# The mean-square sums of an MLP's norm are issued earlier, and rstd and the copies of values out of PSUM get the priority of evacuations

## The chip, the cores and the metric

The kernel runs on one core of a Trainium2 chip. A core has five engines with instruction queues of their own, each served strictly in order: TensorE (PE; its weight loads are shown as PEld), VectorE (DVE), ScalarE (ACT), GpSimd (POOL) and SyncE (SP). They meet only at semaphores. TensorE writes its results to PSUM; VectorE and ScalarE carry them from there to SBUF (an "evacuation"). The metric is the device time of one execution in microseconds, lower is better.

## The reference

Two request groups share one set of weights: a context pass of 128 tokens and a denoising step of 512. The kernel handles them as T = 640 columns. There are two layers (L = 2), D = 1024, and each layer is

```
h = rmsnorm(x, g_attn) * (1 + scale1) + shift1
q, k, v, gq, gk, gv, gate, zf, zb = split(h @ w_in)
o_na  = attention(q, k, v)                 # neighbourhood window and cached context
o_gla = gla(gq, gk, gv, zf, zb)            # gated linear attention, both directions
x = x + gate1 * (concat(o_na, rmsnorm(o_gla) * silu(gate)) @ w_o)
h = rmsnorm(x, g_mlp) * (1 + scale2) + shift2
x = x + gate2 * (relu(h @ w_up) ** 2 @ w_down)

rmsnorm(x, g) = x * rsqrt(mean(x * x) + eps) * g
```

The factor rsqrt(mean(x * x) + eps) of a token is called rstd below. Arithmetic is float32: each operand of a large product is split into a high and a low part (`wh`, `wl` for weights; two tiles per slice of activations), and three matmuls stand for one.

## The kernel before, in words

Activations lie with features on the 128 partitions and the 640 tokens in the free dimension; x is eight slices `kc` of [128, 640]. Weights come in units of [128, 1024] through a few SBUF buffers: a DMA, ScalarE's copy to `wh`, and the subtraction to `wl` on VectorE or GpSimd (`prefetch`, `prepare`).

**What sets the order.** TensorE's program is in the order in which the code issues it. A small driver (`Drv`) interleaves tasks: the main loop is a `filler` that yields after each slice of a projection, and side tasks (generators) run between its steps. A task can yield a time in us or a claim on buffers ("sm", 2); `Drv` counts TensorE's estimated time `t` and runs a task when its time has come. `Est` keeps estimates of when other engines will have written a tile, and `est.until(tile)` is the estimated rest of that time plus 0.60. The other engines are ordered by a scheduler that takes instructions by priority; `tc.high_priority(offset=self.EVP)` with EVP = 600 moves what is issued inside it ahead of work issued up to 600 places earlier, as far as dependencies allow. Evacuations of projections are issued like that.

**PSUM.** The pool "mm" has two buffers of two banks (`ps_mm`), the pool "sm" four of one bank (`ps_sm`, `ps_ss`). An accumulation can begin only when a buffer's last reader is done.

**The norm before the MLP** (lines 881 to 926). Each finished slice of x goes through `late_chunk`: it is multiplied by a per-feature factor G and split in two parts (`row`, `m`), and its square is added to `lsqa` (in rows: `sqa`). The factor rstd is applied only behind the up projection: `late_stat` sums `lsqa` over the partitions by two matmuls with ones (`ps_ss`), and ScalarE makes rstd by Ln and Exp (`lrstd`, in rows `rstd`). Meanwhile `proj_two` runs the first two up units side by side through both `ps_mm` buffers: for each slice kc six matmuls of the one and six of the other (called a block each, below); behind the last slices comes the evacuation `r<-ps_mm,rstd`, which needs rstd. The third up unit needs a `ps_mm` buffer.

In layer 1 the up units from the fourth on are computed by a scheme of seven half-size products for a pair of units (`proj_pair`), which needs sums of blocks of h: `blocks_begin` (line 1655) makes them on VectorE and ScalarE just then (in rows `r<-r`, `T`, `row<-r,row`; "the block sums").

**The attention's values** (`v_task`, lines 1389 to 1415). Behind each of four value projections p, ScalarE writes `gt`, TensorE transposes it into one `ps_sm` buffer (four transposes) and then into another (two), and VectorE copies both to `V`: one 128x512 copy and two of 64x128. Beside that runs `gla_pair`, whose levels 64, 32, 16, 8, 4, 2, 1 each need a pair of factors from `level_vec` (VectorE: two subtractions `ex<-PN`; ScalarE: an exponential; VectorE: a product `ex<-ex,qk`), 80 small matmuls into two or four `ps_sm` buffers (`ps_sm<-ex`), and copies from there (`A`, `Dg`). Both share the four "sm" buffers. In layer 0, VectorE also carries the modulation's matrix-vector products (`junk<-wr,cbc`, `wr<-wr,cbc`).

All instructions of the engines are recorded by one helper, so that rows of the profile name line 198; they are told apart by tiles.

Of the kernel before, what the change touches and what calls it, by code (L numbers as in the profile page):

```python
# [12 lines left out]
AF = mybir.ActivationFunctionType  # L13
# [5 lines left out]
D = 1024  # L19
T = 640  # L20
# [192 lines left out]
class Kern:  # L213
# [684 lines left out]
    def late_chunk(self, x, kc, rows):  # L898
        nc = self.nc
        hh, hl = rows[kc]  # L900
        for r, a, b in ((1, 0, NS), (0, NS, T)):
            g = self.G[:, kc, r:r + 1]
            nc.scalar.activation(out=hh[:, 2 + a:2 + b], in_=x[kc][:, a:b], func=AF.Copy, scale=g)
            nc.vector.scalar_tensor_tensor(out=hl[:, 2 + a:2 + b], in0=x[kc][:, a:b], scalar=g, in1=hh[:, 2 + a:2 + b].bitcast(F32),
                                           op0=ALU.mult, op1=ALU.subtract)
        if kc == 0:
            nc.scalar.activation(out=self.lsqa, in_=x[kc], func=AF.Square)
        else:
            sq = self.npl.tile([128, T], F32, name="sq")
            nc.scalar.activation(out=sq, in_=x[kc], func=AF.Square)  # L910
            nc.vector.tensor_tensor(out=self.lsqa, in0=self.lsqa, in1=sq, op=ALU.add)
        if kc == KC - 1:
            self.dv.spawn(self.late_stat(), self.est.until(self.lsqa) + 3.0)

    def late_stat(self):
        nc, dv = self.nc, self.dv
        yield ("sm", 2)
        ps = [self.smp.tile([128, 512], F32, name="ps_ss", tag="sm") for _ in range(2)]
        for t, (lo, hi) in zip(ps, self.HALF):
            nc.tensor.matmul(t[:, 0:hi - lo], lhsT=self.ones, rhs=self.lsqa[:, lo:hi], start=True, stop=True)  # L920
        dv.pe(1.07)
        for t, (lo, hi) in zip(ps, self.HALF):
            nc.scalar.activation(out=self.lrstd[:, 2 + lo:2 + hi], in_=t[:, 0:hi - lo], func=AF.Ln, scale=1.0 / D, bias=self.eps)
        dv.rel("sm", 2, self.est.free(*ps))
        nc.scalar.activation(out=self.lrstd[:, 2:2 + T], in_=self.lrstd[:, 2:2 + T], func=AF.Exp, scale=-0.5)
        self.lready = True


# [460 lines left out]
    def v_task(self, l, p, ps):  # L1389

        nc, gp, dv = self.nc, self.gp, self.dv
        t = gp.tile([128, T], F32, name="gt", tag="tmp", bufs=5)
        nc.scalar.activation(out=t[:, :NS].rearrange("p (c r) -> p c r", r=8),
                             in_=ps[0][0][:, :NS].rearrange("p (r c) -> p c r", r=8), func=AF.Copy)
        nc.scalar.activation(out=t[:, NS:T], in_=ps[0][0][:, NS:T], func=AF.Copy)
        nc.scalar.dma_start(out=self.o["new_v"][l, p], in_=t[:, NS:T])
        yield self.est.until(t)
        yield ("sm", 1)
        pt = self.smp.tile([128, 512], F32, name="ps_sm", tag="sm")
        for i in range(3):  # L1400
            nc.tensor.transpose(pt[:, 128 * i:128 * i + 128], t[:, 64 + 128 * i:192 + 128 * i], self.ident)
        nc.tensor.transpose(pt[:, 384:512], t[:, NS:T], self.ident)
        dv.pe(0.43)
        nc.vector.tensor_copy(self.V[:, 0:4, 128 * p:128 * p + 128], pt.rearrange("p (c d) -> p c d", c=4))
        dv.rel("sm", 1, self.est.free(pt))
        yield ("sm", 1)
        pt = self.smp.tile([128, 512], F32, name="ps_sm", tag="sm")
        nc.tensor.transpose(pt[:, 0:128], t[:, 0:128], self.ident)
        nc.tensor.transpose(pt[:, 128:256], t[:, 384:512], self.ident)
        dv.pe(0.22)  # L1410
        for i, hs in enumerate((slice(0, 64), slice(64, 128))):
            nc.vector.tensor_copy(self.V[hs, 4, 128 * p:128 * p + 128], pt[hs, 128 * i:128 * i + 128])
        dv.rel("sm", 1, self.est.free(pt))
        dv.rel("gt")

# [486 lines left out]
```

## Time and profile before

| | |
|---|---|
| median of 3 runs | 1676.16 us (1676.02 to 1676.85) |
| the profiled execution's own time | 1676.12 us |
| its span, first to last instruction | 1674.3 us |
| TensorE busy, matmuls / weight loads | 1609.2 us (96%) / 1538.1 us (92%) |
| VectorE busy | 1226.0 us (73%) |
| ScalarE busy | 749.1 us (45%) |
| GpSimd busy | 388.8 us (23%) |
| mean granted TensorE clock | 0.990 of full speed |

The table gives shares of the whole. It says that TensorE is nearly always at work, and not where it waits; for that one reads the table of waits and then the timeline of the places it names. In the timeline a row is a run of like instructions: start, length, engine, line, operation, tiles, count, and in brackets the idle time of the engine before it and what ended that.

### The profile page before, as it was taken

How to read it: one execution, taken by the hardware profiler on the slowest of the kernel's cores; microseconds unless marked ns; L12 is line 12 of the kernel's file. 1: busy time of each engine (PE TensorE's matmuls, PEld its weight loads, DVE VectorE, ACT ScalarE, POOL GpSimd, SP SyncE). 2: the span in 40 equal slices, each digit the busy share in tenths (PEclk: the TensorE clock that was granted, in tenths of full speed). 3: DMA queues.
4: the chain of work that ended last, by engine and by line, in shares of the span. 5: the costliest groups of instructions: out<-in, count | busy, mean ns of one | idle time of the engine just before them, and what ended most of it. 6: DMA issues, size and time to landing. Idle time of an engine off the chain costs nothing. (4 is left out here: it accounts for less than half of the span.)

```text
span 1674.3 us, 32585 instructions
## 1 busy us (share of the span) xinstructions
PE 1609.2 (96%) x13544; PEld 1538.1 (92%) x13544; DVE 1226.0 (73%) x2318; ACT 749.1 (45%) x1224; POOL 388.8 (23%) x155
## 2 busy tenths in 40 slices
PE   8999899999999999999999998999979999999998
PEld 6988788879999999999998898988979999999998
DVE  5697978888888778777578867578695565665753
ACT  4546345644523323332355373566465344343441
POOL 1100000013344444444300000000222334243341
PEclk9999999999999999999999999999999999999999
DMA  9122242433554445444251111313111223222232
GB/s 373 57 81 79 99 150 76 134 112 99 183 164 140 150 149 166 134 132 151 82 186 51 57 52 50 104 61 108 51 55 60 79 73 101 65 87 76 76 94 84
DMA packets 61347, 179.28 MB, mean 107 GB/s; under 512 B 6928, under 2 KB 17808, under 8 KB 61200
## 3 DMA queue, kind: packets, MB, share of 16 engines
q1 hardware_dynamic: 45360, 159.76, 28.7%
q10 hardware_dynamic: 15840, 17.45, 3.4%
q8 instruction: 107, 1.75, 0.4%
q14 instruction: 40, 0.33, 0.1%
HBM read 170.36 MB, written 6.82 MB: 106 GB/s over the span
## 5 line engine op out<-in xcount | busy, mean ns | idle before, releaser
L198 POOL TENSOR_TENSOR wl<-wr,wh 128x1024 fp32r<-128x1024 f32 (+1 forms) x138 | 375.1, 2724 | 1219.6 <-ACT wh L198 1219.6
L198 PE MATMUL ps_mm<-row,wh 128*128 128x256 f32 (+2 forms) x2192 | 439.3, 320 | 17.9 <-DVE r L198 9.7
L198 ACT ACTIVATE wh<-wr 128x1024 fp32r<-128x1024 f32 (+1 forms) x209 | 215.1, 1029 | 485.3 <-PE ps_sm L198 278.0
L198 PEld LDWEIGHTS ps_mm<-row,wh 128*128 128x128 f32 x2192 | 356.3, 191 | 38.9 <-issue 13.3
L198 PE MATMUL ps_mm<-row,wl 128*128 128x256 f32 (+2 forms) x1096 | 255.5, 312 | 0.5 <-DVE wl L198 0.5
L198 PEld LDWEIGHTS ps_mm<-row,wl 128*128 128x128 f32 x1096 | 200.3, 191 | 0.7 <-DVE wl L198 0.7
L198 PE MATMUL ps_sm<-row,wh 128*128 128x322 f32 (+2 forms) x736 | 153.6, 312 | 0.0
L198 ACT ACTIVATE r<-r 128x512 f32<-128x512 f32 (+2 forms) x192 | 113.6, 618 | 63.3 <-DVE r L198 60.5
L198 DVE SCALAR_TENSOR_TENSOR ar<-ar,cbc 128x1024 f32<-128x1024 f32 x56 | 125.0, 2239 | 1.0
L198 PEld LDWEIGHTS ps_sm<-row,wh 128*128 128x128 f32 x736 | 122.1, 189 | 0.0
L198 PE MATMUL ps_mm<-uh,wh 128*128 128x256 f32 (+1 forms) x512 | 118.8, 308 | 0.0
L198 PE MATMUL ps_mm<-ul,wh 128*128 128x256 f32 (+1 forms) x512 | 118.5, 307 | 0.0
L198 PE MATMUL ps_sm<-ul,wh 128*128 128x256 f32 (+1 forms) x512 | 118.4, 307 | 0.0
L198 PE MATMUL ps_mm<-uh,wl 128*128 128x256 f32 (+1 forms) x512 | 118.4, 307 | 0.0
L198 PE MATMUL ps_sm<-uh,wl 128*128 128x256 f32 (+1 forms) x512 | 118.4, 307 | 0.0
L198 PE MATMUL ps_sm<-uh,wh 128*128 128x256 f32 (+1 forms) x512 | 118.4, 307 | 0.0
L198 DVE SCALAR_TENSOR_TENSOR row<-ps_sm,mod,row 128x256 f32<-128x256 f32 (+1 forms) x216 | 81.8, 432 | 49.2 <-PE ps_sm L198 49.2
L198 DVE TENSOR_TENSOR r<-ps_sm,r 128x322 f32<-128x322 f32 x98 | 46.9, 491 | 93.5 <-PE ps_sm L198 55.7
L198 DVE TENSOR_TENSOR wl<-wr,wh 128x1024 fp32r<-128x1024 f32 (+2 forms) x74 | 81.2, 1098 | 44.8 <-ACT wh L198 44.2
L198 DVE SCALAR_TENSOR_TENSOR row<-ps_mm,mod,row 128x128 f32<-128x128 f32 (+2 forms) x180 | 89.6, 536 | 30.2 <-PE ps_mm L198 30.1
L198 PE MATMUL ps_sm<-m,wh 128*128 128x322 f32 x480 | 99.2, 312 | 0.0
L198 PE MATMUL ps_sm<-row,wl 128*128 128x322 f32 (+2 forms) x368 | 98.9, 311 | 0.0
(222 smaller groups left out, 3038.2 us busy)
## 6 DMA issues: line engine op xcount, KB each, us to landing
wr<-w_dn SPq DMA_DIRECT2D x68, 512.0 KB, 3.5
wr<-w_up SPq DMA_DIRECT2D x64, 512.0 KB, 3.5
ar<-w_ada SPq DMA_DIRECT2D x56, 512.0 KB, 3.7
wr<-w_in SPq DMA_DIRECT2D x48, 512.0 KB, 3.9
wr<-w_ada SPq DMA_DIRECT2D x24, 512.0 KB, 3.6
wa<-w_ada SPq DMA_DIRECT2D x16, 512.0 KB, 10.2
wr<-w_o SPq DMA_DIRECT2D x16, 512.0 KB, 3.5
tab<-bias ACTq DMA_DIRECT2D x32, 96.0 KB, 3.0
```

Of the source, the lines that this page charges most:

```text
L198: r = f(*args, **kw)
```

## The change

Three things are edited, and no instruction is added or removed:

- `late_chunk` starts the task `late_stat` at `est.until(lsqa)` instead of 3.0 us (of the driver's time) later.
- `late_stat`'s Ln and Exp on ScalarE are issued with the priority of evacuations.
- `v_task`'s copies from PSUM to `V` on VectorE are issued with the priority of evacuations.

```diff
         if kc == KC - 1:
-            self.dv.spawn(self.late_stat(), self.est.until(self.lsqa) + 3.0)
+            self.dv.spawn(self.late_stat(), self.est.until(self.lsqa))
...
         dv.pe(1.07)
-        for t, (lo, hi) in zip(ps, self.HALF):
-            nc.scalar.activation(out=self.lrstd[:, 2 + lo:2 + hi], in_=t[:, 0:hi - lo], func=AF.Ln, scale=1.0 / D, bias=self.eps)
-        dv.rel("sm", 2, self.est.free(*ps))
-        nc.scalar.activation(out=self.lrstd[:, 2:2 + T], in_=self.lrstd[:, 2:2 + T], func=AF.Exp, scale=-0.5)
+        with self.tc.high_priority(offset=self.EVP):
+            for t, (lo, hi) in zip(ps, self.HALF):
+                nc.scalar.activation(out=self.lrstd[:, 2 + lo:2 + hi], in_=t[:, 0:hi - lo], func=AF.Ln, scale=1.0 / D, bias=self.eps)
+            dv.rel("sm", 2, self.est.free(*ps))
+            nc.scalar.activation(out=self.lrstd[:, 2:2 + T], in_=self.lrstd[:, 2:2 + T], func=AF.Exp, scale=-0.5)
         self.lready = True
...
-        nc.vector.tensor_copy(self.V[:, 0:4, 128 * p:128 * p + 128], pt.rearrange("p (c d) -> p c d", c=4))
+        with self.tc.high_priority(offset=self.EVP):
+            nc.vector.tensor_copy(self.V[:, 0:4, 128 * p:128 * p + 128], pt.rearrange("p (c d) -> p c d", c=4))
...
         for i, hs in enumerate((slice(0, 64), slice(64, 128))):
-            nc.vector.tensor_copy(self.V[hs, 4, 128 * p:128 * p + 128], pt[hs, 128 * i:128 * i + 128])
+            with self.tc.high_priority(offset=self.EVP):
+                nc.vector.tensor_copy(self.V[hs, 4, 128 * p:128 * p + 128], pt[hs, 128 * i:128 * i + 128])
```

What this does to the order of instructions shows at three places. A minus marks a row of before, a plus one of the change; a number behind a name is a tile's own.

TensorE, layer 1, in the first two up units; the slices come in the order row 0 to 7, then m, each twice (once per unit):

```order
 L198 MATMUL ps_mm<-row_5_13350,wh 128x322 x2
 L198 MATMUL ps_mm<-row_4_13349,wl 128x322 x2
+L198 MATMUL ps_ss<-sqa,ones 128x256
+L198 MATMUL ps_ss<-sqa,ones 128x384
 L198 MATMUL ps_mm<-row_6_13351,wh 128x322 x2
 L198 MATMUL ps_mm<-row_7_13352,wh 128x322 x2
```

The two sums stand behind the third slice now; before, they stood four blocks (two slices of both units) further on. In layer 0 they move up to the same place, also by four blocks.

VectorE, layer 1, at the end of the same two units; `row_4` to `row_7` are the last block sums, `r<-ps_mm,rstd` is the evacuation of an up unit:

```order
 L198 TENSOR_TENSOR row_4_13708<-r,row_4_13708 128x322
-L198 TENSOR_TENSOR r<-r 128x322 x2
+L198 TENSOR_TENSOR r<-r 128x322
 L198 TENSOR_TENSOR row_6_13710<-r,row_6_13710 128x322
+L198 TENSOR_TENSOR r<-ps_mm,rstd_4524 128x644
+L198 TENSOR_TENSOR r<-r 128x322
 L198 TENSOR_TENSOR row_5_13709<-r,row_5_13709 128x322
-L198 TENSOR_TENSOR row_7_13711<-r,row_7_13711 128x322
-L198 TENSOR_TENSOR r<-ps_mm,rstd_4524 128x644 x2
+L198 TENSOR_TENSOR r<-ps_mm,rstd_4524 128x644
 L198 TENSOR_TENSOR wr<-wr 128x512
```

The first unit's evacuation has moved ahead of one subtraction and of the products of `row_5` and `row_7`, the second's ahead of `row_7`. On ScalarE, Ln and Exp have moved from among the copies of `row_4` to `row_7` to a place some ten instructions earlier.

VectorE, layer 1, where the first two value projections' copies meet the levels of `gla_pair`:

```order
 L198 COPY A<-ps_sm 128x512
-L198 TENSOR_TENSOR ex<-PN 128x640 x2
-L198 TENSOR_TENSOR ex<-ex,qk 128x1280 x2
 L198 COPY V<-ps_sm 128x4x128
 L198 COPY V<-ps_sm 64x128 x2
+L198 TENSOR_TENSOR ex<-PN 128x640
 L198 COPY V<-ps_sm 128x4x128
-L198 TENSOR_TENSOR ex<-PN 128x640 x2
+L198 TENSOR_TENSOR ex<-ex,qk 128x1280
 L198 COPY V<-ps_sm 64x128 x2
+L198 TENSOR_TENSOR ex<-PN 128x640 x3
 L198 TENSOR_TENSOR ex<-ex,qk 128x1280
```

The copies to `V` stand directly behind the copy `A` now, ahead of two levels' subtractions and products. In layer 0 they move forward in the same way, there past modulation products too. TensorE's order doesn't change at the value projections of either layer, and the order on GpSimd and of the DMAs on SP doesn't change anywhere.

## Rows read from the trace of the kernel before

**Rows 1.** The page: the span, and busy time, share and instructions of each engine.

```profile
span 1674.3 us, 32585 instructions
PE 1609.2 (96%) x13544; PEld 1538.1 (92%) x13544; DVE 1226.0 (73%) x2318; ACT 749.1 (45%) x1224; POOL 388.8 (23%) x155
```

**Rows 2.** The table of TensorE's waits over the whole span: who waited, for whom, us in total, times, longest.

```profile
PE ps_mm L198 <- DVE r L198: 9.7, 1, 9.7
...
PE ps_sm L198 <- DVE V L198: 4.4, 2, 3.2
```

**Rows 3.** Timeline of TensorE in layer 1, the first two up units (to 1247.88), the third (from 1257.56) and the fourth (from 1267.11).

```profile
1237.71 0.75 PE L198 MATMUL ps_mm<-row,wh 128*128 128x322 f32 x4
...
1241.28 1.24 PE L198 MATMUL ps_ss<-sqa,ones 128*128 128x256 f32 x4
...
1247.42 0.46 PE L198 MATMUL ps_mm<-m,wl 128*128 128x322 f32 x2
1257.56 1.44 PE L198 MATMUL ps_mm<-row,wh 128*128 128x322 f32 x4 [9.68 <-DVE r L198]
...
1267.11 0.76 PE L198 MATMUL ps_sm<-row,wh 128*128 128x322 f32 x4
```

**Rows 4.** Timeline of VectorE at the same place: the last addition to `sqa`, the last block sums, the two evacuations.

```profile
1239.85 0.82 DVE L198 TENSOR_TENSOR sqa<-sqa,sq 128x640 f32<-128x640 f32 x1
...
1249.92 1.02 DVE L198 TENSOR_TENSOR r<-r 128x322 f32<-128x322 f32 x2
1250.86 0.49 DVE L198 TENSOR_TENSOR row<-r,row 128x322 fp32r<-128x322 f32 x1
1251.83 4.93 DVE L198 TENSOR_TENSOR row<-r,row 128x322 fp32r<-128x322 f32 x2 [0.49 <-ACT row L198]
1256.69 1.55 DVE L198 TENSOR_TENSOR r<-ps_mm,rstd 128x644 f32<-128x644 f32 x2
```

**Rows 5.** Timeline of ScalarE (the copy of `row_6`, rstd's Exp) and of GpSimd (two weights' low parts) at the same place.

```profile
1250.02 0.47 ACT L198 ACTIVATE row<-r 128x322 fp32r<-128x322 f32 x1
...
1252.05 0.73 ACT L198 ACTIVATE rstd<-rstd 128x640 f32<-128x640 f32 x1
...
1251.52 4.90 POOL L198 TENSOR_TENSOR wl<-wr,wh 128x1024 fp32r<-128x1024 f32 x2 [13.27 <-ACT wh L198]
```

**Rows 6.** Stretches of the span: from:to, length, busy time (and instructions) of PE, PEld, DVE, ACT and POOL, then the granted clock of TensorE as a share of full speed (1.00 is 2.4 GHz, 0.50 is 1.2 GHz), the DMAs' share and GB/s.

```profile
198.00:201.20 3.20, 3.20 (x23) 3.16 (x13) 3.15 (x7) 1.58 (x2) 0.00 (x0) 0.51 0.02 5
...
1024.30:1027.20 2.90, 2.90 (x13) 2.90 (x12) 2.27 (x5) 1.24 (x2) 0.00 (x0) 0.51 0.00 0
...
1257.60:1262.50 4.90, 4.90 (x18) 4.90 (x19) 3.01 (x5) 4.49 (x8) 0.00 (x0) 0.50 0.02 5
...
1274.00:1670.00 396.00, 395.90 (x2716) 395.64 (x2714) 237.95 (x394) 160.39 (x216) 149.79 (x59) 1.00 0.26 82
```

**Rows 7.** Timelines of TensorE and then VectorE in layer 1, where the second value projection's transposes meet the level 8 (1019.65 and 1023.14), the level 4 (1028.41) and the level 2 (1032.08).

```profile
1023.14 0.89 PE L198 MATMUL ps_sm<-ex 64*32 64x32 f32 x72 [3.23 <-DVE V L198]
...
1024.30 1.41 PE L198 MATMUL ps_mm<-row,wh 128*128 128x256 f32 x4
...
1028.41 0.89 PE L198 MATMUL ps_sm<-ex 64*32 64x32 f32 x80
1029.23 0.85 PE L198 MATMUL ps_mm<-row,wh 128*128 128x256 f32 x4
...
1032.08 0.89 PE L198 MATMUL ps_sm<-ex 64*32 64x32 f32 x80
...
1022.40 1.90 DVE L198 COPY V<-ps_sm 128x512 f32<-128x512 f32 x4
...
1032.95 0.57 DVE L198 COPY_PREDICATED Dg<-masks,ps_sm 128x160 f32<-128x160 int32 x2 [2.71 <-PE ps_sm L198]
```

**Rows 8.** Timelines of TensorE and then VectorE in layer 0, at the second value projection's transposes (191.97) and the level 2 (195.83 and 197.22).

```profile
191.97 0.63 PE L198 MATMUL ps_sm<-ident,gt 128*128 128x128 f32 x4 [2.07 <-DVE Dg L198]
...
195.83 0.26 PE L198 MATMUL ps_sm<-ex 64*32 64x32 f32 x8 [1.25 <-DVE ex L198]
197.22 0.89 PE L198 MATMUL ps_sm<-ex 64*32 64x32 f32 x72 [1.13 <-DVE V L198]
...
187.33 1.23 DVE L198 TENSOR_TENSOR wl<-wr,wh 128x1024 fp32r<-128x1024 f32 x1 [0.77 <-ACT wh L198]
...
194.28 1.49 DVE L198 TENSOR_TENSOR ex<-ex,qk 128x1280 f32<-128x1280 f32 x1
195.69 0.98 DVE L198 TENSOR_TENSOR ex<-PN 128x640 f32<-128x640 f32 x1
196.57 0.60 DVE L198 COPY V<-ps_sm 64x128 f32<-64x128 f32 x2
```

**Rows 9.** Timelines of layer 0's first two up units: TensorE's first block behind the third slice, and VectorE's last addition to `sqa` and its two evacuations; last, GpSimd at the second evacuation.

```profile
417.09 0.75 PE L198 MATMUL ps_mm<-row,wh 128*128 128x322 f32 x4
...
417.22 0.81 DVE L198 TENSOR_TENSOR sqa<-sqa,sq 128x640 f32<-128x640 f32 x1
425.60 0.83 DVE L198 TENSOR_TENSOR r<-ps_mm,rstd 128x644 f32<-128x644 f32 x1 [7.57 <-PE ps_mm L198]
427.31 0.83 DVE L198 TENSOR_TENSOR r<-ps_mm,rstd 128x644 f32<-128x644 f32 x1 [0.88 <-PE ps_mm L198]
...
426.41 5.78 POOL L198 TENSOR_TENSOR wl<-wr,wh 128x1024 fp32r<-128x1024 f32 x2 [9.93 <-ACT wh L198]
```

## The prediction

> **What bounds the kernel now.** The page says that TensorE computes 96% of the span [rows 1], so what can be gained is its waits and the stretches at half clock behind them. Next comes the table of TensorE's waits: its largest entry is one wait of 9.7 us for `r`, an evacuation, and among the next is one of 3.2 us for `V` [rows 2]. Both lie in layer 1. The third view is the timeline at each; what to see there is which instruction ended the wait and what stood before it on its engine. The fourth is the table of stretches: behind both waits the granted clock is 0.50 to 0.51, 1.2 of 2.4 GHz [rows 6]. From 1274 to 1670 TensorE is busy 395.90 of 396.00 us [rows 6], so what is won or lost before arrives at the end in full.
>
> The sum is made against the profiled execution, 1676.12 us: a span of 1674.3 and 1.8 around it, 0.04 under the median of the runs. No instruction is added or removed and no DMA changes its place on SP; every term is a wait.
>
> **Layer 1, the 9.7 us (main term).** The first two up units end at 1247.88 and the third starts at 1257.56 [rows 3], when the first of two evacuations (1.55 us together, from 1256.69) has freed a buffer [rows 4]. Its input rstd was there at 1252.78 [rows 5]. What held it is VectorE's queue: the products of `row_5` and `row_7`, 4.93 us in place of some 0.5 each [rows 4], beside GpSimd's two weight parts, 1251.52 to 1256.42 [rows 5].
>
> Now the evacuation stands behind `row_6`. That ended at 1251.35 with two subtractions ahead of it (1.02 us together) [rows 4]; one is now behind, so it ends near 1250.9. TensorE restarted 0.87 us after the evacuations began (1256.69 to 1257.56), so now at 1251.8. Rstd is no longer late: its sums come as below, and Ln and Exp now stand ahead of `row_6`'s copy on ScalarE instead of around it.
>
> The sums themselves now meet a wait. They stand four blocks earlier, where the next block began at 1237.71 [rows 3], but the last addition to `sqa` ends at 1240.67 [rows 4] and nothing in the order of VectorE up to there has moved. TensorE waits some 3.0 us, and behind it in its queue stand ten blocks. The two units then end near 1250.9 (1247.88 + 3.0), the first some two blocks (1.8 us) sooner, near 1249.1, before VectorE is free for it. So this wait is hidden by the evacuation's, at no cost; with the clock at half after it the units would end up to 1.7 us later, near 1252.6, and that costs 0.8.
>
> The gap shrinks to some 0.9 us, and I take it that the third unit runs at full clock: four blocks take 3.57 us (1237.71 to 1241.28), eight 7.14, against 9.55 before (1257.56 to 1267.11) [rows 3]. It ends at 1251.8 + 7.1 = 1258.9 in place of 1267.1: **-8.2 us**. Bounds: -4.7 (restart as late as 1255.3, full clock) and -9.0 (VectorE reaches the evacuation 0.8 sooner).
>
> What VectorE does behind the evacuation is still held by GpSimd, now with the second evacuation behind it, near 1256.5; the second buffer is not wanted by then, since the fourth unit uses `ps_sm` [rows 3].
>
> **Layer 1, the 3.2 us.** Level 8 wants two `ps_sm` buffers; one was free, the other was held by a transposed value tile until VectorE's copy, which began at 1022.40 behind two levels' subtractions and products [rows 7]. Now the copy follows `A`, some 4 us sooner, before TensorE comes to level 8. The 3.23 us go, and so does the low clock behind them: the three blocks from 1024.30 took until 1028.41 (4.11 us), those from 1029.23 until 1032.08 (2.85), a difference of 1.26 [rows 7]. Together **-4.5 us**. What is late next is level 2's product, one group of copies (1.25 us: 1.90 for two 128x512 and two 64x128 copies [rows 7], 0.60 for two more 64x128 [rows 8], halved) and one subtraction later than now; it is due only after level 4, and VectorE still has an idle 2.71 us at 1032.95 [rows 7]. Bounds: 0 and -4.5.
>
> **Layer 0, the sums.** The same move by four blocks. TensorE comes there at 417.09, the last addition ends at 417.22 + 0.81 = 418.03 [rows 9]: a wait of 1.0 with the semaphore. Nothing hides it: VectorE's first evacuation waits for TensorE (7.57 us idle) and not for rstd [rows 9], so TensorE's whole queue moves back. **+1.05 us**. Bounds: +0.8 and, with a stretch at half clock such as the 1.26 above, +2.3.
>
> **Layer 0, the copies.** The waits of 2.07, 1.25 and 1.13 us [rows 8] look like those of layer 1, but VectorE is busy 3.15 of 3.20 us behind them [rows 6] and all around. The first wait goes (a copy frees the buffer sooner). The next ones don't: level 2's product, at 194.28 to 195.77, now has three more 64x128 pairs or 128x512 copies ahead of it (0.60 each) and one more subtraction (0.88, from 195.69 to 196.57), 2.68 in all, of which 0.77 fill an idle place at 187.33 [rows 8]. It ends at 197.7, and TensorE goes on 0.5 later than at 197.22, after one long wait in place of three. The low clock (0.51 from 198.0 to 201.2 [rows 6]) stays or lasts longer. I take **+0.7**. Bounds: +1.8 (0.5 and one more 1.26) and -4.5 (all three waits go). The copies of the third and fourth projection keep their places or nearly.
>
> **Sum.** -8.2 - 4.5 + 1.05 + 0.7 = -10.95, and 1676.12 - 10.95 = **1665.2 us**. Its own range is 1663 to 1668.
>
> The Trainium skill ("SBUF — State Buffer", section "Who interferes with whom") says that a VectorE instruction with two SBUF inputs and a GpSimd one that reads SBUF keep each other out, whichever starts first holding the ports for its whole length, and that with at most one SBUF input there is no contention. The trace agrees: two products with two SBUF inputs took 4.93 us beside GpSimd's 4.90, while an evacuation with one input in PSUM took 0.83 inside GpSimd's 5.78 from 426.41 [rows 4, 5, 9]. By that rule the moved evacuation is not held itself, but what stands right ahead of it can be; that is the first rival.
>
> **Rivals.**
> - *The product of `row_6` is held by GpSimd.* It starts near 1250.4, GpSimd near 1251.4. If GpSimd comes first, the product waits out the first weight part (half of 4.90, to 1253.97), ends at 1254.4, and TensorE restarts at 1255.3 after a gap of 4.4 with the clock at half (1.26 lost): 4.7 - 1.3 = 3.4 gained in place of 8.2, **1670.0 us**. For it: the two products just behind were held so [rows 4]. Against it: the copy of `row_6` precedes the weight's high part on ScalarE, which GpSimd waits for [rows 5].
> - *The freed wait in the levels comes back at the next one,* VectorE being what they wait for: -8.2 + 1.75 = -6.45, **1669.7 us**. For it: VectorE came to the copies at 1022.40 without an idle moment. Against it: its idle 2.71 a little later [rows 7].
> - *The main gap only changes its reason* (the third unit then waits for something else until 1257.6): -4.5 + 1.75, **1673.4 us**, within 0.2%. Against it: nothing later than the evacuation appears in the table of waits.
> - *Slower: copies ahead of the level chain cost TensorE their own length.* In both layers the levels wait for VectorE, and each of eight groups of copies (four a layer) puts 1.25 us ahead of a product. If each is waited out, that is +10.0, with no wait saved and one more half-clock stretch (1.26): -8.2 + 1.05 + 10.0 + 1.3 = +4.1, **1680.3 us**. It decides from 10.5 us in all (7.15 to eat the net gain, 3.35 for 0.2%). For it: the 1.25 us wait for `ex` in layer 0 [rows 8]. Against it: only the first two groups of a layer move past a product.
>
> That the change does nothing is excluded by the order, which differs at all places.
>
> **How the numbers follow.** A measurement of this kernel can tell 0.2%, 3.35 us, from no change: faster is below 1672.8, slower above 1679.5. Chances: the forecast 0.64, row_6 held 0.12, levels wait again 0.11, main gap remains 0.09, slower 0.04. Faster 0.64 + 0.12 + 0.11 = 0.87, same 0.09, slower 0.04. The range takes in the first three and reaches below for the bound of layer 0's copies: 1661.5 to 1670.5.
>
> **What would show it.** In the trace after: TensorE's wait for `r` under 2 us and the granted clock at 1.00 in the third up unit; two new waits on `sqa`, near 1.0 us in layer 0 and 3.0 in layer 1; no wait for `V` in layer 1 and full clock behind level 8; in layer 0 one wait of 4 to 5 us before level 2. The prediction is wrong if the third up unit starts more than 2 us behind the end of the second, or if level 4 or 2 in layer 1 finds TensorE waiting for `ex`.

## The result, and the profile after

The changed kernel takes 1668.29 us (median of 4 runs, 1666.73 to 1671.75), the kernel before 1676.27 (4 runs, 1676.02 to 1676.85): a ratio of 0.995, 95% interval 0.9936 to 0.9965, faster by more than 0.2%. The time lies in the predicted range, 3.1 us above the predicted figure. The profiled execution took 1666.83 us. Its span is 9.3 us shorter than that of the profile before (1674.3 to 1665.0), and the rows below are there to account for those 9.3 us. Of the runs of the kernel before that stand beside the experiments below, two took 2110 and 3114 us; they count as slow and are left out of every comparison.

The page of the changed kernel, to compare with [rows 1]:

```profile
span 1665.0 us, 32591 instructions
...
PE 1607.2 (97%) x13544; PEld 1536.2 (92%) x13544; DVE 1226.5 (74%) x2318; ACT 749.4 (45%) x1224; POOL 388.3 (23%) x155
```

TensorE does the same matmuls. Its busy time falls by 2 us, with a mean granted clock of 0.993 in place of 0.990; the rest of the gain is idle time. Its table of waits, to compare with [rows 2] (us in total, times, longest):

```profile
PE ps_sm L198 <- DVE ex L198: 9.6, 3, 4.0
...
PE ps_ss L198 <- DVE sqa L198: 3.7, 2, 2.8
...
PE ps_mm L198 <- DVE r L198: 0.7, 1, 0.7
```

The 9.7 us for `r` are 0.7, and no wait for `V` is left. New are two on `sqa`, 3.7 us in all, of which the longer is layer 1's 2.8; and the waits for `ex`, 6.3 us before, have grown to 9.6. Where that is, the timelines show. TensorE in layer 1, to compare with [rows 3]: the block behind which the sums now stand, the sums, the end of the first two up units, the third unit and the fourth.

```profile
1235.63 0.75 PE L198 MATMUL ps_mm<-row,wh 128*128 128x322 f32 x4
...
1239.51 1.34 PE L198 MATMUL ps_ss<-sqa,ones 128*128 128x256 f32 x4 [2.83 <-DVE sqa L198]
...
1249.36 0.46 PE L198 MATMUL ps_mm<-m,wl 128*128 128x322 f32 x2
1250.53 0.86 PE L198 MATMUL ps_mm<-row,wh 128*128 128x322 f32 x4 [0.71 <-DVE r L198]
...
1257.81 0.76 PE L198 MATMUL ps_sm<-row,wh 128*128 128x322 f32 x4
```

The same block before:

```profile
1236.82 0.75 PE L198 MATMUL ps_mm<-row,wh 128*128 128x322 f32 x4
```

From the block to the fourth unit it is now 22.18 us (1235.63 to 1257.81); before it was 30.29 (1236.82 to 1267.11 [rows 3]), so 8.1 us are gained here. VectorE at that place, to compare with [rows 4], and below it ScalarE's Exp and GpSimd, to compare with [rows 5]:

```profile
1249.25 0.48 DVE L198 TENSOR_TENSOR row<-r,row 128x322 fp32r<-128x322 f32 x1
1249.65 0.82 DVE L198 TENSOR_TENSOR r<-ps_mm,rstd 128x644 f32<-128x644 f32 x1
1250.39 2.41 DVE L198 TENSOR_TENSOR r<-r 128x322 f32<-128x322 f32 x1
1252.72 2.69 DVE L198 TENSOR_TENSOR row<-r,row 128x322 fp32r<-128x322 f32 x1
1255.33 0.82 DVE L198 TENSOR_TENSOR r<-ps_mm,rstd 128x644 f32<-128x644 f32 x1
```

```profile
1243.15 0.74 ACT L198 ACTIVATE rstd<-rstd 128x640 f32<-128x640 f32 x1
...
1250.05 5.01 POOL L198 TENSOR_TENSOR wl<-wr,wh 128x1024 fp32r<-128x1024 f32 x2 [13.02 <-ACT wh L198]
```

The first evacuation comes 7.0 us earlier, 1.2 of which the whole place is earlier. What GpSimd holds now (a subtraction of 2.41 and a product of 2.69 us, in place of 0.49 each) stands behind it, and the second evacuation, at 1255.33, is not missed: the fourth unit uses `ps_sm`.

TensorE at layer 1's values, to compare with [rows 7]; the second row is the next group of transposes that both kernels have:

```profile
1021.12 0.87 PE L198 MATMUL ps_sm<-ident,gt 128*128 128x128 f32 x6 [1.17 <-ACT A L198]
...
1035.22 0.88 PE L198 MATMUL ps_sm<-ident,gt 128*128 128x128 f32 x6
```

It is 14.10 us from the one to the other, and no row between them shows a wait. Layer 0's values, TensorE and then VectorE, to compare with [rows 8]: the first transposes, the level behind them, level 2 and level 1; on VectorE the copies to `V` that now stand ahead.

```profile
182.36 0.60 PE L198 MATMUL ps_sm<-ident,gt 128*128 128x128 f32 x4
185.81 0.89 PE L198 MATMUL ps_sm<-ex 64*32 64x32 f32 x80 [2.85 <-DVE ex L198]
...
198.65 1.08 PE L198 MATMUL ps_sm<-ex 64*32 64x32 f32 x80 [4.01 <-DVE ex L198]
...
204.53 0.89 PE L198 MATMUL ps_sm<-ex 64*32 64x32 f32 x80
...
183.67 0.69 DVE L198 COPY V<-ps_sm 128x512 f32<-128x512 f32 x1
...
193.78 0.59 DVE L198 COPY V<-ps_sm 64x128 f32<-64x128 f32 x2 [0.41 <-PE ps_sm L198]
```

The first transposes, the level behind them and level 1 before:

```profile
182.29 0.60 PE L198 MATMUL ps_sm<-ident,gt 128*128 128x128 f32 x4
185.19 0.89 PE L198 MATMUL ps_sm<-ex 64*32 64x32 f32 x80 [2.30 <-DVE ex L198]
...
202.26 0.89 PE L198 MATMUL ps_sm<-ex 64*32 64x32 f32 x80
```

Here TensorE loses. The wait behind the first transposes grows from 2.30 to 2.85 us. The three waits of [rows 8] are one, 4.01 us long, that ends 1.4 us later than the last of them did (198.65 for 197.22), and level 1, at 202.26 before, comes at 204.53, 2.3 us later. The stretches show the clock there and, in the last two rows, at the two places of layer 1 (columns as in [rows 6]):

```profile
187.00:190.00 3.00, 3.00 (x14) 3.00 (x13) 2.87 (x5) 1.37 (x5) 0.00 (x0) 0.52 0.16 22
199.70:204.00 4.30, 4.30 (x18) 4.30 (x17) 4.27 (x10) 1.74 (x3) 0.00 (x0) 0.50 0.01 4
1024.50:1029.00 4.50, 4.50 (x106) 4.26 (x106) 4.47 (x7) 1.37 (x2) 0.00 (x0) 1.00 0.02 5
...
1250.60:1257.80 7.20, 7.20 (x48) 7.20 (x49) 6.75 (x5) 3.43 (x7) 4.46 (x2) 1.00 0.22 74
```

In layer 1 both places run at full clock (before, 0.51 and 0.50 [rows 6]). In layer 0 the clock is at half behind both waits, for over 4 us behind the second.

So the span's 9.3 us are, from place to place: layer 0's values +2.3, layer 0's sums +1.2 (a wait of 0.88 on `sqa` and the semaphore), layer 1's values -4.9, layer 1's gap -8.1 (the sum, -9.5, leaves 0.2 for all other places).

### The profile page after: what moved, and what is told of

Its sections match the earlier page's. It is cut to its first block, busy times and chain, and to the rows that moved or that the text cites. A ratio compares the mean times of both kernels' runs of the same rounds, so it can differ in the third digit from the quotient of the medians.

```text
span 1665.0 us, 32591 instructions
## 1 busy us (share of the span) xinstructions
PE 1607.2 (97%) x13544; PEld 1536.2 (92%) x13544; DVE 1226.5 (74%) x2318; ACT 749.4 (45%) x1224; POOL 388.3 (23%) x155
```

## The experiments

They ran on two chips, each beside the kernel before: the first four on one (median of before 1676.5 us, 27 runs from 1670.7 to 1680.3), the others on a second (1677.1, 20 runs from 1672.2 to 1686.1). Single runs spread far more there than the four of the first measurement, so that a median of some ten is good to about 2 us. Each ratio is to the runs of before on the same chip, and the microseconds behind it are the ratio's; the two medians alone can differ from it by about 1 us.

**The norm's part alone.** The copies to `V` as before:

```diff
-        with self.tc.high_priority(offset=self.EVP):
-            nc.vector.tensor_copy(self.V[:, 0:4, ...
+        nc.vector.tensor_copy(self.V[:, 0:4, ...
```

> Only the norm's part of the change (early sums, Ln and Exp at the priority of evacuations); the copies to V stand as before. Theory (the terms add up as the two traces show them: layer 1's gap -8.1, layer 0's sums +1.2, layer 1's V wait -4.8, layer 0's copies +2.4): -6.9 against the kernel before, about 1669.3 us; the wait for V of 3.2 us in layer 1 is back, layer 0 looks as before up to its sums, then TensorE meets a wait on sqa near 1 us. Rival A (the 9.7-us wait went only because the moved copies changed VectorE's queue further up): the wait for r stays over 5 us and the time is within 3 us of the kernel before. Rival B (layer 0's loss belongs to the norm, not to the copies): -4.5, about 1671.7 us.

Measured: 1672.31 us (11 runs), ratio 0.9975 (0.9962 to 0.9988), that is -4.2 us (-6.4 to -2.0). The expected -6.9 is just outside, rival B's -4.5 is inside; the medians alone don't choose. The trace does on the place: the wait for `r` is 0.74 us, the block ahead of the sums is at 1237.32 and the fourth unit at 1259.49, 22.17 us as in the changed kernel. So rival A is out. Rival B is out by layer 0's values, which take the time of before (the comparison stands with layer 0's copies, below). Two rows of its trace show layer 1's values without the change:

```profile
1017.95 0.87 PE L198 MATMUL ps_sm<-ident,gt 128*128 128x128 f32 x6 [1.17 <-ACT A L198]
...
1036.99 0.88 PE L198 MATMUL ps_sm<-ident,gt 128*128 128x128 f32 x6
```

That is 19.04 us, in place of 14.10. The pair repeats in every profile: 19.00 to 19.06 where the copies stand as before (five), 14.08 to 14.10 where they are ahead (five). Layer 1's V term is -4.9 us.

**The copies alone.** The norm's edits undone:

```diff
-            self.dv.spawn(self.late_stat(), self.est.until(self.lsqa))
+            self.dv.spawn(self.late_stat(), self.est.until(self.lsqa) + 3.0)
-        with self.tc.high_priority(offset=self.EVP):
+        with self.tc.high_priority(offset=0):
```

> Only the copies to V at the priority of evacuations; the norm as before. Theory (terms of the two traces): -4.8 in layer 1 and +2.4 in layer 0, so -2.4 against the kernel before, about 1673.8 us; the wait for r in layer 1 is back near 9.7 us. If the wide spread of the changed kernel's times (1666.7 to 1671.8) belongs to stretches at half clock behind layer 0's copies, this kernel's times spread by some 3 to 5 us too, and those of the norm alone by under 2 us. Rival (layer 0's copies cost only the 0.7 us that I had predicted, the rest being chance of one profile): -4.1, about 1672.1 us.

Measured: 1672.78 us (12 runs, 1668.96 to 1676.63), ratio 0.9976 (0.9965 to 0.9988), -4.0 us (-5.9 to -2.0). Theory and rival both lie inside. The wait for `r` is back at 9.7. On the spread the theory falls: the norm alone, without these copies, spreads over 9.3 us, more than this one's 7.7. The spread is not the copies'. The two parts together make -8.2, as the whole change does when it is run again (below).

**All of it, in layer 1 alone.** Each of the three edits is made to depend on the layer, as here:

```diff
-        with self.tc.high_priority(offset=self.EVP):
+        with self.tc.high_priority(offset=self.EVP if l == 1 else 0):
```

> All parts of the change, but in layer 1 alone; layer 0 as before. Theory (terms of the two traces): -8.1 - 4.8 = -12.9 against the kernel before, about 1663.3 us, 3.6 less than the profiled execution of the changed kernel, and a spread of under 2 us as the kernel before has. Rival A (layer 0's edits as predicted: +1.75 in all): only 1.75 under the changed kernel's best, about 1665.0 us. Rival B (the shift of layer 0 is made up later, so undoing it gains nothing): about 1666.8 us, as the changed kernel's best.

Measured: 1665.49 us (5 runs, 1663.73 to 1666.28), ratio 0.9933 (0.9919 to 0.9946), -11.2 us (-13.6 to -9.1). The theory's -12.9 is inside, and so are rival A's 1665.0 us and rival B's 1666.8, so the time alone doesn't choose. The changed kernel's ratio is 0.9951 when it is run again (below), 3.0 us slower than this one's, but the two intervals overlap. Rival B is out by the traces: what layer 0 loses isn't made up later, since the changed kernel stands 3.6 us behind the kernel before at 870 (874.20 for 870.59) and still at layer 1's values (1021.12 for 1017.52). By its median this kernel is faster than both. Its trace, beside that of the changed kernel, shows where single executions part:

```profile
870.50 0.58 PE L198 MATMUL ps_mm<-row,wh 128*128 128x256 f32 x1 [2.10 <-ACT row L198]
...
883.95 0.44 PE L198 MATMUL ps_mm<-row,wh 128*128 128x384 f32 x1 [0.88 <-ACT row L198]
...
1238.30 1.70 PE L198 MATMUL ps_ss<-sqa,ones 128*128 128x256 f32 x4 [2.85 <-DVE sqa L198]
...
1257.19 0.76 PE L198 MATMUL ps_sm<-row,wh 128*128 128x322 f32 x4
```

And at the first of these places the kernel before's first row and both of the changed kernel's:

```profile
870.59 0.39 PE L198 MATMUL ps_mm<-row,wh 128*128 128x256 f32 x1 [2.10 <-ACT row L198]
...
874.20 0.38 PE L198 MATMUL ps_mm<-row,wh 128*128 128x256 f32 x1 [2.10 <-ACT row L198]
...
885.07 0.44 PE L198 MATMUL ps_mm<-row,wh 128*128 128x384 f32 x1 [0.88 <-ACT row L198]
```

The wait is the same 2.10 us, in a part of the program that no edit touches. In the one execution a matmul behind it takes 0.58 us, in the other 0.38, and the same work takes 13.45 and 10.87 us: 2.6 us, because the clock fell behind the same wait once and not the other time. In seven of the ten profiles of this study the stretch takes 10.86 to 10.88 us, in three 12.3 to 13.5. The second pair shows the forecast's hidden wait at its limit: the clock fell behind the wait on `sqa` (0.50 from 1239.3 to 1242.0), the two units ended later, and the third found its buffer free at once; the stretch from block to fourth unit (1234.41 to 1257.19) is 22.78 us, 0.6 more, where the forecast put this case at 0.8.

**Only Ln and Exp at the priority of evacuations.** On the kernel before, so sums late and copies as before:

```diff
-        for t, (lo, hi) in zip(ps, self.HALF):
-            nc.scalar.activation(out=self.lrstd[:, 2 + lo:2 + hi], ...
+        with self.tc.high_priority(offset=self.EVP):
+            for t, (lo, hi) in zip(ps, self.HALF):
+                nc.scalar.activation(out=self.lrstd[:, 2 + lo:2 + hi], ...
...
```

> Only Ln and Exp at the priority of evacuations; the sums stay four blocks late and the copies to V as before. TensorE's order is then that of the kernel before. Theory (what ended the 9.7-us wait is the evacuation's place in VectorE's queue, not the place of the sums): the wait for r falls under 2 us with no wait on sqa, -8 to -9 in layer 1 and nothing in layer 0, about 1667.6 us; against the norm's whole part 1.2 us faster. Rival (rstd is late without the early sums, so the evacuation waits for it): the gap stays at 2 to 5 us with the clock at half behind it, -3 to -5, about 1672 us.

Measured: 1670.42 us (12 runs), ratio 0.9970 (0.9957 to 0.9983), -5.0 us (-7.2 to -2.9). The theory's -8 to -9 is outside; the time lies at the rival's end, and so does the wait for `r`, 3.66 us. But what ended the wait is only in part what the rival says. VectorE ahead of the evacuation, and then ScalarE's Exp:

```profile
1255.33 0.49 DVE L198 TENSOR_TENSOR row<-r,row 128x322 fp32r<-128x322 f32 x1 [0.49 <-ACT row L198]
...
1256.53 0.49 DVE L198 TENSOR_TENSOR r<-r 128x322 f32<-128x322 f32 x1 [0.30 <-ACT r L198]
1256.94 0.82 DVE L198 TENSOR_TENSOR r<-ps_mm,rstd 128x644 f32<-128x644 f32 x1
...
1254.21 0.73 ACT L198 ACTIVATE rstd<-rstd 128x640 f32<-128x640 f32 x1
```

The Exp ended at 1254.94; the evacuation stands behind block sums, two of which waited for ScalarE (0.49 and 0.30 us), where Ln and Exp now come ahead of their inputs. What ends TensorE's wait here is VectorE's queue, as before, without GpSimd's hold. Rstd sets a floor all the same: TensorE restarts 0.9 us after the evacuation begins, so with rstd at 1254.94 the third unit could not have started before 1255.8, which is 1.7 us of the 3.66. The idle time is that of the changed kernel, in one piece: 3.66, against 2.83 + 0.71 = 3.54 there. Behind it the clock fell, and the stretch from the same block (1243.10) to the fourth unit (1266.58) took 23.48 us: in this execution 6.8 of the 8.1 us come from the place of the evacuation alone. (With the sums early, on the other hand, the priority of Ln and Exp adds nothing: the changed kernel's program is the same, instruction by instruction, with and without it. So in the changed kernel the early sums alone move the evacuation ahead, and with late sums the priority moves it, though behind more block sums.)

**Layer 1 alone, sums late.** As the layer-1 kernel, but the sums stay four blocks late:

```diff
-  ... self.est.until(self.lsqa) + (0.0 if self.lsq_l == 1 else 3.0))
+  ... self.est.until(self.lsqa) + 3.0)
```

> Layer 1 alone has the copies to V and Ln and Exp at the priority of evacuations; the sums stay four blocks late, layer 0 is as before, and TensorE's order is as before but for the levels of layer 1. Theory (the idle time in front of the third up unit is the same with early sums, 2.8 on sqa + 0.7 on r = 3.5, as with late ones, one wait of 3.7 on r): the time is that of the change in layer 1 alone within 2 us, 11 under the kernel before by the medians, near 1665.5 us. Rival (early sums are worth something of their own, since two short waits let the clock fall less often than one long one): 1.3 to 3 us slower than the change in layer 1 alone, 1667 to 1668.5 us, with the clock at half in the third up unit.

Measured: 1665.75 us (6 runs, 1663.23 to 1668.83), ratio 0.9928 (0.9910 to 0.9946), -12.1 us (-15.1 to -9.1). By the medians the theory holds: no difference to the sums early (-11.2 on the other chip). Beside the changed kernel itself, on the same chip, its median is 2.7 us lower (1668.47 below), though the two intervals overlap. The rival's sign is in the trace all the same, TensorE's third unit and then the clock behind its wait:

```profile
1244.93 1.44 PE L198 MATMUL ps_mm<-row,wh 128*128 128x322 f32 x4 [3.64 <-DVE r L198]
...
1245.00:1250.00 5.00, 5.00 (x19) 5.00 (x20) 5.00 (x3) 3.12 (x6) 5.00 (x2) 0.50 0.28 87
```

From the block at 1230.23 to the fourth unit at 1254.67 it is 24.44 us, 2.3 over the changed kernel's 22.18. What early sums give in layer 1 is thus up to 2.3 us in an execution, and not settled by six runs.

**Layer 0's copies alone.** All else as before:

```diff
-        with self.tc.high_priority(offset=self.EVP):
+        with self.tc.high_priority(offset=self.EVP if l == 0 else 0):
```

> Only layer 0's copies to V at the priority of evacuations; all else as before. It measures the term that I had put at +0.7 us. Theory (in the changed kernel the level in front of the fourth projection pair comes 2.3 us later, since VectorE's chain of subtractions and products is what bounds these levels and each copy put ahead lengthens it): +2.0 to +2.7 us against the kernel before, near 1678.8 us if that has its median of 1676.5 on this chip. Rival A (my +0.7 was right and the 2.3 was where the clock happened to fall): within 1 us of the kernel before. Rival B (the copies cost their length at each of four groups): +5 us.

Measured: 1679.89 us (12 runs), ratio 1.0012 (0.9996 to 1.0027), +2.0 us (-0.7 to +4.5). The theory's figure; rival A is inside the interval, rival B outside. The traces decide, by three rows: the transposes, level 2 and level 1.

```profile
178.92 0.60 PE L198 MATMUL ps_sm<-ident,gt 128*128 128x128 f32 x4
...
194.81 0.88 PE L198 MATMUL ps_sm<-ex 64*32 64x32 f32 x80 [4.06 <-DVE ex L198]
...
199.98 0.89 PE L198 MATMUL ps_sm<-ex 64*32 64x32 f32 x80
```

And the same three of layer 1 alone with late sums, where layer 0 is as before:

```profile
179.02 0.60 PE L198 MATMUL ps_sm<-ident,gt 128*128 128x128 f32 x4
...
193.74 0.82 PE L198 MATMUL ps_sm<-ex 64*32 64x32 f32 x72 [1.13 <-DVE V L198]
...
197.32 0.89 PE L198 MATMUL ps_sm<-ex 64*32 64x32 f32 x80
```

21.06 and 18.30 us. Over all profiles: with the copies ahead 20.58 to 22.17 (mean 21.25, four), without 18.17 to 19.97 (mean 18.83, six): +2.4 us. In two halves: to level 2 it is 15.51 to 16.29 with and 14.52 to 14.93 without (means 15.93 and 14.75, +1.2); from there to level 1 it is 5.07 to 5.88 with, and without it is 3.57 or 3.58 four times and 5.04 and 5.13 twice (means 5.33 and 4.08, +1.2). The second half is the clock: behind one wait of 4 us it fell all four times, behind the three shorter waits two times in six.

**One of GpSimd's parts given to VectorE.** On the kernel before; the part then stands behind the evacuations (the edit moves a like part that follows, too, further on):

```diff
-        eng = nc.vector if q % 2 else nc.gpsimd
+        eng = nc.vector if q % 2 or j == self.units.index(("up", 1, 4)) else nc.gpsimd
```

> The kernel before, with one of the two weight parts that GpSimd makes beside the products of row_5 and row_7 in layer 1 given to VectorE, where it stands behind the two evacuations (and the like part that follows, later on); all in front of the evacuations keeps its order. Theory (the two products took 4.93 us because GpSimd held them): one product takes some 2.5 us and the other 0.5, the evacuation comes 1.9 to 2.0 us earlier, and TensorE's wait for r falls from 9.7 to 7.6 to 7.9 us. Rival (the products wait for something else, as their inputs from ScalarE): the wait stays at 9.7 us within 0.3.

Measured: 1671.2 us in a single run, too little to compare times; the wait for `r` is 7.51 us. TensorE, VectorE and GpSimd:

```profile
1253.00 1.44 PE L198 MATMUL ps_mm<-row,wh 128*128 128x322 f32 x4 [7.51 <-DVE r L198]
...
1249.41 2.79 DVE L198 TENSOR_TENSOR row<-r,row 128x322 fp32r<-128x322 f32 x2 [0.49 <-ACT row L198]
...
1249.10 2.35 POOL L198 TENSOR_TENSOR wl<-wr,wh 128x1024 fp32r<-128x1024 f32 x1 [13.26 <-ACT wh L198]
```

The two products take 2.79 us in place of 4.93 [rows 4], and the wait is 2.2 us shorter: the products were held by GpSimd, one by each part. The rival is out. But the hold is not the whole of the long wait. In the kernel before, rstd was ready at 1252.78, and TensorE restarted 0.87 us after the evacuation began; so even without the hold the third unit could not have started before 1253.65, 5.8 us behind the end of the first two (1247.88 [rows 3]). The hold accounts for the last 3.9 us of the 9.7, and rstd's lateness alone would have left 5.8. In the changed kernel rstd is ready at 1243.89, long before the evacuation.

**The changed kernel again.** No edit.

> The changed kernel once more, unchanged, beside the others on the same chip. Theory (its waits are set by its order and repeat, while whether the clock falls behind a wait of 2 to 4 us differs from run to run): waits on sqa, r and ex within 0.3 us of those of the first profile, stretches at half clock in partly other places, times spread over 5 us or more, and a median 7 to 9 us under the kernel before. Rival (the first profile was a lucky order of events): waits differ by over 1 us.

Measured: 1668.47 us (9 runs, 1663.84 to 1673.42), ratio 0.9951 (0.9933 to 0.9970), -8.2 us (-11.2 to -5.0). The median and the spread (9.6 us) are as the theory says. The waits on `sqa` (3.7 in all, 2.8 the longest) and on `r` (0.73) repeat. The one on `ex` doesn't, against the theory:

```profile
184.08 0.60 PE L198 MATMUL ps_sm<-ident,gt 128*128 128x128 f32 x4
187.53 0.89 PE L198 MATMUL ps_sm<-ex 64*32 64x32 f32 x80 [2.85 <-DVE ex L198]
...
199.59 0.95 PE L198 MATMUL ps_sm<-ex 64*32 64x32 f32 x80 [4.77 <-DVE ex L198]
```

Behind the first wait, again 2.85 us, the clock stayed at 1.00 this time (188 to 191), TensorE came to the second transposes sooner, VectorE found them ready (no 0.41 us of idle before the copies) and reached level 2's product sooner: 15.51 us from the transposes to level 2, against 16.29 in the first profile.

## Why the prediction was right, and where it was not

- **The main term, layer 1's gap: -8.2 predicted, -8.1 in the trace.** By its steps: a wait of 2.83 on `sqa` (predicted 3.0), the evacuation directly behind `row_6`'s product, a gap of 0.71 (0.9), the third unit at full clock. Two things made the long wait, and both went. GpSimd's hold on the products ahead of the evacuation is shown by taking half of it away (2.2 us); by the rows it is the last 3.9 of the 9.7 us. The rest is the late rstd, which the forecast names only as no longer late. GpSimd's hold has these numbers: each held instruction took 2.3 to 2.7 us, about one part of GpSimd's 2.35 to 2.5, and the evacuation at 1249.65, which GpSimd's start at 1250.05 overlaps, took its 0.82. The rule of the Trainium skill ("SBUF — State Buffer", "Who interferes with whom") that the first to start holds the ports for its whole length agrees with them. By the run times the term is rather smaller: the norm alone, less layer 0's sums, gives -4.2 - 1.2 = -5.4; layer 1 alone, less its values, -11.2 + 4.9 = -6.3. Both have an uncertainty of some 2 us; whether 1 or 2 us of the trace's 8.1 are given back in other executions stays open.
- **Layer 1's values: -4.5 predicted, -4.9 measured.** Both the wait and the half clock behind it went, and nothing took their place.
- **Layer 0's sums: +1.05 predicted, +1.2 measured.** Nothing hid the wait.
- **Layer 0's copies: +0.7 predicted, +2.4 measured.** This term was mis-sized, and lies past its upper bound of 1.8. The one long wait came as predicted (4.0 to 4.8 us), and where the clock stayed up behind the first wait (the changed kernel again) level 2 came 0.6 us later than before (15.51 for 14.93), as the step's +0.5 says. What the step left out is that the first copy, 0.69 us, goes ahead of an earlier level's product too: that lengthens a wait from 2.3 to 2.85, and the clock fell behind it in three of four profiles. Behind such a fall TensorE brings the second transposes later (11.0 us after the first in the changed kernel's first profile, 9.5 where the clock stayed up), and VectorE, with the copy now at the head of its queue, idled for them in two of the three (0.41 us, and 0.33 with the copies alone). And "the low clock stays or lasts longer" was taken at nothing and should have been the +1.2 that a fall in every profile costs over a fall in two of six.
- **The rivals.** `row_6`'s product was not held (0.48 us, over 0.3 us before GpSimd began). The levels of layer 1 did not wait again. The slower rival's mechanism is at work in layer 0, at 2.4 us instead of its 5 a layer, and not in layer 1, where VectorE has idle time behind the levels.
- **The sum.** -8.1 - 4.9 + 1.2 + 2.4 = -9.4; the profiled execution gave -9.3, and 1666.83 us. The medians, 1668.3 and 1668.5, lie higher. In runs without a trace a longer time goes with a lower granted clock (the changed kernel again: 1663.84 us at 0.995, 1673.42 at 0.988), so the executions seem to differ by the falls of the clock. The profiled one had 0.993, the other three of its measurement 0.988 to 0.990; that it came within 1.6 us of the forecast is in part luck.

## What to carry to other kernels

Putting a buffer's release ahead in a queue paid here where the engine behind it had idle time afterwards (layer 1) and cost where that engine's chain was itself the bound (layer 0): the same edit gave -4.9 and +2.4 us. The two kernels that keep the change to layer 1 have the lowest times here (1665.5 us, the median of their 11 runs, against 1668.5 of the changed kernel's 13). When one wait has several causes, work out what each alone would leave: GpSimd's hold was the one that ended last in the wait of 9.7 us, but the late rstd alone would have left 5.8. When a wait of TensorE changes by half a microsecond, or three waits become one, ask what the clock does behind it; that was worth as much as the wait. And before a change is judged by a few per mille, look at how far single executions of the kernel before spread: four of them agreed to 0.8 us, and twenty others spread over 14.

## What the runs showed of the hardware that was not expected

One and the same wait may or may not cost a stretch at half clock. Over the ten profiles the clock fell behind the 2.10 us wait at 870 in three of ten, behind layer 0's 2.3 us wait in four of six, behind the waits of 2.8 us (on `sqa` in layer 1, and layer 0's lengthened one) in four of eight, and behind the waits of 3.2 us and more in layer 1's values and in front of the third up unit every time. In layer 0's values without the copies ahead, each of the six profiles has exactly one fall, behind the 2.3 us wait (four) or behind level 2's (two). In one place a fall cost 2.6 us (13.45 for 10.87), in another nothing, because a later wait shrank by as much: where the clock fell behind layer 0's 2.3 us wait, the next wait was 0.5 to 0.7 us in place of 1.7 to 2.1, and the clock stayed up behind level 2, so that the stretch took 18.2 to 18.5 us in place of 19.7 to 20.0. So the kernel's time differs from run to run by several microseconds, though the order of its work and most of its waits are the same.
